# The rows of a gather and the gate products of one Trainium2 core's expert layer: a fixed order between them on VectorE, fetches paced by copied row numbers, and gate reads queued behind tile loads

## The chip, the cores and the metric

The kernel runs on one of the eight cores of a Trainium2 chip. The metric is the device time of one execution in microseconds (us), here the median of several runs. A core has five engines with a queue each: TensorE (PE in the profile, with its weight loads PEld), VectorE (DVE), ScalarE (ACT), GpSimd (POOL) and SyncE (SP). An engine works through its own queue in order; engines wait for each other by semaphores. Transfers are issued from the queues of SP, ACT and POOL.

## The reference

One layer of a decoder with 512 tokens of width 1024: an mLSTM and sliding-window attention mixer, cross-attention into 256 memory tokens, and a product-key expert layer. Only the last matters here. Each of 8 heads takes its best 16 of 128 x 128 single-neuron experts:

```python
u = expert_down[eidx]                                  # (token, head, 16, D)
a = gelu(einsum('thkd,td->thk', u, xb))
coef = softmax(top_s) * a
out = einsum('thk,thkd->td', coef, expert_up[eidx])
```

There are 16384 experts, each a row of 1024 numbers in `expert_down` and one in `expert_up`; 8 x 16 = 128 of them are chosen for a token. The layer's result is added to the residual, and a final RMSNorm gives the output. Everything is float32.

## The kernel before, in words

The 512 tokens are four blocks of 128. The kernel handles two kinds of block differently.

*Blocks 1 to 3 (384 tokens) go through all experts.* The 16384 experts are 128 tiles of 128. A "down tile" (class `Down`, lines 812 to 859) loads the tile's rows (`draw`, two tiles per transfer, line 820), splits them on ScalarE into a rounded part `dh` (line 785) and on VectorE into a remainder `dl` (line 823), multiplies in 24 matmuls (lines 834 to 836) and takes a gelu. An "up step" (`up_tile` and `up_mm`, lines 862 to 909) multiplies that gelu with the gates: it loads the tile of `expert_up` (`uraw`, line 876), splits it into `uh` (ScalarE, line 785) and `ul` (VectorE, line 886), forms the product `cf` of gelu and gates on VectorE (line 893), splits the product into `ch` (ScalarE, line 895) and `cl` (VectorE, line 896), and accumulates 18 matmuls (lines 907 to 909) into six banks that stay open over all 128 steps. All these working tiles have two buffers. The first SP = 72 down tiles are made early, among the routing and the gating, and are spilled to memory (`gd`); seven more (LEAD) are made between the gating and the up steps; the other 49 are made among the up steps, at a rate that `made_by` sets, so that a step has none or one of them. With FREE = 3 the matmuls of a down tile may not be queued ahead of those of the up step three before.

*The gates* are a table of token by expert in memory, `wd`, one per block. For block 1 GpSimd adds 128 columns into it, one indirect transfer each (`scatter`, line 685). For blocks 2 and 3 the function `gating` (lines 694 to 750) builds it on chip: for 32 groups q of four tokens, one-hot matrices come from VectorE (line 739) and ScalarE, TensorE multiplies them (line 740), ScalarE copies the result into a staging tile `stg` (line 742, two buffers), and after every eighth group ScalarE's queue stores it (line 744, 2 MB each). The early down tiles' matmuls run between. An up step reads the gates of four tiles at a time as `wt`, in three transfers from SP's queue (line 868), one for each block.

*Block 0 (128 tokens) gathers its rows.* For each of its 128 (head, rank) pairs j, GpSimd fetches 128 rows, one for each token, by an indirect transfer (line 762, 512 KB). `gather` (lines 753 to 779) is a generator of 256 rounds: the first 128 fetch from `expert_down` and take a dot product on VectorE (line 768), then the coefficients are formed, and 128 more fetch from `expert_up` and add to `gacc` on VectorE (line 778). Below, a "row" is one such round, numbered 0 to 255, and its VectorE instruction is the "row operation". Rows use eight buffers, so a fetch waits for the row operation eight before. The row numbers come from `eidx`, or from its copy `rowid` after LEAD.

*What sets the order.* The program is built by a scheduler that fixes each engine's queue ahead of time. Among instructions that its own timeline holds to be ready it takes the one that the program names first. `issue_after(x)` forces the instructions of one engine that follow in its block to be queued behind x on that engine; it is an order and no semaphore. By hand, 12 rows are placed in the gating of block 3 (at q = 9, 11, ... 31, set GQ), 10 in LEAD (GLD), and the other 234 among the up steps: line 1185 gives each step a due number, 3 for a step plus 5 for each down tile made, and line 1186 shares the rows out in proportion, up to step GST - 1 = 119. A row's operation is queued behind the step's product (the first row) or behind its `cl` (the others), which bounds it on one side alone: nothing forces it ahead of later steps.

After the last step, `finish` (lines 912 to 927) adds `gacc` (block 0) and the open banks (blocks 1 to 3) to the residual, takes the norm on VectorE, ScalarE and GpSimd, and stores the output. The last two steps' matmuls are taken block by block.

Of the kernel before, what the change touches and what calls it, by code (L numbers as in the profile page):

```python
# [21 lines left out]
P = 128  # L22
# [18 lines left out]
UG = 4  # L41
# [8 lines left out]

GQ = range(9, 32, 2)
GLD = 10
GST = 120
WST, WTL = 3, 5


# [637 lines left out]
def gating(c, early, ga):  # L694

    nc, ps, gs, mp = c.nc, c.ps, c.gs, c.mp
    V, A, T = nc.vector, nc.scalar, nc.tensor
    for b in range(NG + NS, NB):
        tr = []
        for n_, src in (("I1T", c.I1), ("I2T", c.I2), ("gT", c.gg)):  # L700
            tp = ps.tile([P, 512], F32, tag="a", name="tp_i")
            tr_ = T.transpose(tp[:, :P], src[:, b].rearrange("p h k -> p (h k)"), c.ident)
            o = gs.tile([P, P], F32, tag=n_, bufs=1, name=n_)
            A.copy(o, tp[:, :P])
            tr.append(o)
        i1, i2, g = tr
        n1 = gs.tile([P, P], F32, tag="n1", bufs=1, name="n1")
        A.mul(n1, i1, -1.0)
        io = c.iota.unsqueeze(1).to_broadcast([P, 4, P])

        def onehot(q):

            o1 = gs.tile([P, 4, P], F32, tag="oh1", bufs=5, name="oh1")
            ib = i1[:, 4 * q:4 * q + 4].unsqueeze(2).to_broadcast([P, 4, P])
            if q % 2:
                V.tensor_tensor(o1, io, ib, op=ALU.is_equal)
            else:
                for t1 in range(4):
                    t = 4 * q + t1
                    A.activation(o1[:, t1], c.iota, AF.Abs, bias=n1[:, t:t + 1])  # L720
                A.activation(o1, o1, AF.Relu, bias=1.0, scale=-1.0)
            return o1

        oh = [onehot(q) for q in range(3)]
        if b == NG + NS:
            with c.tc.issue_after(tr_.ins):
                early.fill(FGT0)
        for q in range(32):
            if q % 8 == 0:
                stg = gs.tile([P, NK, 32], F32, tag="stg", bufs=2, name="stg")  # L730
            if q + 3 < 32:
                oh.append(onehot(q + 3))
            o1 = oh[q]
            w = ps.tile([P, 512], F32, tag="b", name="w")
            w4 = w.rearrange("p (i t) -> p i t", t=4)
            for t1 in range(4):
                t = 4 * q + t1
                o2 = gs.tile([P, P], F32, tag="oh2", bufs=4, name="oh2")
                last = V.tensor_scalar(o2, c.iota, i2[:, t:t + 1], g[:, t:t + 1], op0=ALU.is_equal, op1=ALU.mult)
                mm = T.matmul(w4[:, :, t1], o1[:, t1], o2, start=True, stop=True)  # L740
            q8 = q % 8
            A.copy(stg[:, :, 4 * q8:4 * q8 + 4], w4)
            if q8 == 7:
                nc.scalar.dma_start(c.wd[b - NG][:, :, 32 * UG * (q // 8):32 * UG * (q // 8 + 1)].rearrange("g p i -> p g i"),
                                  stg.rearrange("p (g i) t -> p g (i t)", i=UG))
            with c.tc.issue_after(mm.ins):
                early.fill(FGT)
            if b == NB - 1 and q in GQ:
                with c.tc.issue_after(c.sc[HD - 1][-1].ins), c.tc.issue_after(last.ins):
                    step(ga, 1)  # L750


def gather(c):

    nc, gp, mp = c.nc, c.gp, c.mp
    V, A, G = nc.vector, nc.scalar, nc.gpsimd
    dots = gp.tile([P, P], F32, name="dots")
    c.gacc = gp.tile([P, D], F32, name="gacc")

    def fetch(src, j):  # L760
        r = gp.tile([P, D], F32, tag="rows", bufs=8, name="rows")
        G.indirect_dma_start(out=r, out_offset=None, in_=src,  # L762
                             in_offset=bass.IndirectOffsetOnAxis(ap=c.rowid[:, j:j + 1], axis=0))
        return r

    for j in range(P):
        r = fetch(c.a["down_r"], j)
        V.tensor_tensor_reduce(r, r, c.xn0, 1.0, 0.0, op0=ALU.mult, op1=ALU.add, accum_out=dots[:, j:j + 1])  # L768
        yield
    coef = gp.tile([P, P], F32, name="coef")  # L770
    A.activation(coef, dots, AF.Gelu)
    V.tensor_tensor(coef, coef, c.gg[:, 0].rearrange("p h k -> p (h k)"), op=ALU.mult)
    for j in range(P):
        r = fetch(c.a["up"], j)
        if j == 0:
            V.tensor_scalar(c.gacc, r, coef[:, j:j + 1], None, op0=ALU.mult)
        else:
            V.scalar_tensor_tensor(c.gacc, r, coef[:, j:j + 1], c.gacc, op0=ALU.mult, op1=ALU.add)  # L778
        yield


def split3(c, pool, raw, tag, bufs):
# [29 lines left out]
class Down:  # L812


    def __init__(self, c, i2):
        nc, dp = c.nc, c.dp
        self.c, self.i2 = c, i2
        if i2 % GRP == 0:
            c.draw = dp.tile([P, GRP, D], F32, tag="draw", bufs=2, name="draw")
            nc.sync.dma_start(c.draw, c.a["down_t"][i2 // GRP])  # L820
        raw = c.draw[:, i2 % GRP]
        self.hi, self.lo = split3(c, dp, raw, "d", 2)
        c.dl = nc.vector.tensor_tensor(self.lo, raw, f32(self.hi), op=ALU.subtract)  # L823
        self.acc = None
        self.k = 0
# [36 lines left out]
def up_tile(c, u, i2, gel, acc):  # L862
    nc, up = c.nc, c.up
    V, A, T = nc.vector, nc.scalar, nc.tensor
    if i2 % UG == 0:
        c.wt = up.tile([P, ND, UG * P], F32, tag="wt", bufs=2, name="wt")
        for b in range(ND):
            i = nc.sync.dma_start(c.wt[:, b], c.wd[b][i2 // UG])
            for j in c.sc[HD - 1] if b == 0 else ():
                c.tc.add_manual_dep(i.ins, j.ins.name, SYNC, reason="gates complete")  # L870
        if i2 < SP:
            c.gsr = c.gl.tile([P, UG, TD], F32, tag="gsr", bufs=2, name="gsr")
            nc.sync.dma_start(c.gsr, c.gd[i2 // UG])
    if i2 % GRP == 0:
        c.uraw = up.tile([P, GRP, D], F32, tag="uraw", bufs=3, name="uraw")
        nc.sync.dma_start(c.uraw, c.a["up"].rearrange("(i p) d -> p i d", p=P)[:, i2:i2 + GRP])
    g = c.gsr[:, i2 % UG] if i2 < SP else gel[i2]
    raw = c.uraw[:, i2 % GRP]
    last = u == NK - 1
    if last:  # L880
        z = c.xlo.rearrange("p k t -> p (k t)")
        hi, lo = z[:, 0:D], z[:, D:2 * D]
        A.copy(hi, raw)
    else:
        hi, lo = split3(c, up, raw, "u", 2)
    V.tensor_tensor(lo, raw, f32(hi), op=ALU.subtract)  # L886
    cf = up.tile([P, TD], F32, tag="cf", bufs=2, name="cf")
    if last:
        ch, cl = z[:, 2 * D:2 * D + TD], z[:, 3 * D:3 * D + TD]
    else:  # L890
        ch = up.tile([P, TD], F32R, tag="ch", bufs=2, name="ch")
        cl = up.tile([P, TD], F32R, tag="cl", bufs=2, name="cl")
    c.cf = V.tensor_tensor(cf.rearrange("p (b t) -> p b t", t=32), g.rearrange("p (b t) -> p b t", t=32),
                    c.wt.rearrange("p b (q i t) -> p (b q) i t", q=4, i=UG)[:, :, i2 % UG], op=ALU.mult)
    A.copy(ch, cf)  # L895
    c.cl = V.tensor_tensor(cl, cf, f32(ch), op=ALU.subtract)  # L896
    return hi, lo, ch, cl
# [206 lines left out]
def body(tc, a, out, dbg=None):  # L1104
# [3 lines left out]
    with ExitStack() as st:  # L1108
# [55 lines left out]
            ws.close()  # L1164
        c.gl = st.enter_context(pool("gels"))
        with pool("gather", side="right") as c.gp:
            c.rowid = c.eidx
            ga = gather(c)
            with pool("gating") as c.gs:
                gating(c, early, ga)  # L1170
            c.up = st.enter_context(pool("up"))
            assert len(gel) == SP

            for n in range(LEAD):
                ahead(1)
                with tc.issue_after(c.dl.ins):
                    step(ga, GLD * (n + 1) // LEAD - GLD * n // LEAD)
            c.rowid = c.gp.tile([P, P], I32, name="rowid")
            with tc.issue_after(c.dl.ins):
                nc.vector.tensor_copy(c.rowid, c.eidx)  # L1180
            pst_ = [c.ps.tile([P, 512], F32, tag=t, name="acc_u") for t in "bbbbaa"]
            acc = [[pst_[2 * b], pst_[2 * b + 1]] for b in range(ND)]
            last, mms = [], []
            g0 = len(GQ) + GLD
            due = [WST * u + WTL * made_by(u) for u in range(-1, GST)]
            rows = [(2 * P - g0) * (d - due[0]) // (due[-1] - due[0]) for d in due]
            rows += [rows[-1]] * (NK - GST)
            for u, i2 in enumerate(up_order()):
# [6 lines left out]
                for i in range(rows[u + 1] - rows[u]):  # L1195
                    with tc.issue_after((c.cf if i == 0 else c.cl).ins):
                        step(ga, 1)
                if u >= NK - 2:
                    last.append(parts)
                else:  # L1200
                    for b in range(ND):
                        up_mm(c, u, parts, acc, b)
                    mms.append(c.mm)
# [34 lines left out]
def step(it, n):  # L1238
    for _ in range(n):
        next(it, None)  # L1240
# [49 lines left out]
```

## Time and profile before

| | us |
|---|---|
| median of 3 runs (1652.19 to 1653.87) | 1652.22 |
| the profiled execution | 1653.3 |
| its span, first to last instruction | 1651.5 |

| engine | busy us | share of the span |
|---|---|---|
| PE | 1609.7 | 97% |
| PEld (beside PE) | 1415.1 | 86% |
| DVE | 1235.1 | 75% |
| ACT | 723.6 | 44% |
| POOL | 591.1 | 36% |

The first 400 us or so are the mixer and the attention, then routing until about 680, the gating until about 870, LEAD until about 900 and the up steps until the end. The granted TensorE clock was 0.989 of full speed over the span. The profile comes from one execution. A timeline line reads: start and length in us, engine, line of the kernel, operation, output<-inputs, shapes, count, and in brackets the idle time just before with what ended it. A group line gives the count, busy us, mean ns of one, and the idle time of the engine before them. A wait line gives who waited for whom, the total in us, how often, and the longest. In the chain of waits each line is a start, a length and what the end of the program hung on then. SPq marks the time an instruction stood at the head of SyncE's queue.

### The profile page before, as it was taken

To read this page: it belongs to the slowest core of one execution; us is meant where nothing else is said; L and a number is where in the kernel's file an instruction comes from. 1 tells how busy PE (TensorE), PEld (TensorE's weight loads), DVE (VectorE), ACT (ScalarE), POOL (GpSimd) and SP (SyncE) were. 2 spreads that over 40 slices of the span, in tenths; PEclk is the share of its full clock that TensorE was granted. 3 is DMA by queue.
4 is the path that set the end of the run, shared out by engine and by line. 5 is a ranking of instruction groups with operands and counts; after the bars stand their busy time and mean duration, and the time that the engine had idled before them with its cause. 6 is when DMAs were issued, how large, how long until landed. Compare 5 with 4: busy or idle time off the path is not lost.

```text
span 1651.5 us, 23090 instructions
## 1 busy us (share of the span) xinstructions
PE 1609.7 (97%) x8388; PEld 1415.1 (86%) x8388; DVE 1235.1 (75%) x2704; ACT 723.6 (44%) x1217; POOL 591.1 (36%) x427
## 2 busy tenths in 40 slices
PE   8998899999999999999999999999999999999994
PEld 5776688878999999999998888888888888888883
DVE  5546564464787887777796888788888888888898
ACT  5445544342544454678664333333333333333332
POOL 2000000000027787877221543444433434334451
PEclk9999999999999999999999999999999999999997
DMA  5236134232254435678999999999989889988895
GB/s 214 77 127 255 59 126 173 77 153 106 96 168 145 116 71 141 181 190 213 342 305 339 410 393 347 343 342 338 334 335 367 338 321 333 362 317 320 323 364 181
DMA packets 151122, 402.17 MB, mean 244 GB/s; under 512 B 28368, under 2 KB 62304, under 8 KB 138848
## 3 DMA queue, kind: packets, MB, share of 16 engines
q1 hardware_dynamic: 58208, 240.04, 39.0%
q0 software_dynamic: 55360, 134.32, 24.8%
q10 hardware_dynamic: 37440, 26.35, 5.1%
q8 instruction: 66, 1.08, 0.3%
q14 instruction: 48, 0.39, 0.1%
HBM read 357.07 MB, written 43.58 MB: 243 GB/s over the span
## 4 chain that ended last, share of the span: by engine, by line
PE 89%; DVE 4%; DMA 3%; ACT 2%; issue 1%; POOL 0%; DVEq 0%; SPq 0%; POOLq 0%; ACTq 0%
PE acc_u L907 10%; PE acc_u L908 10%; PE acc_u L909 10%; PE acc_d L836 10%; PE acc_d L834 10%; PE acc_d L835 10%; PE acc_f L1008 4%; PE acc_f L1009 4%; PE acc_f L1010 4%; PE w L740 3%; DMA wd<-stg 3%; PE acc_t L1023 2%; PE acc_t L1022 2%; PE acc_t L1021 2%; DVE gacc L778 1%
## 5 line engine op out<-in xcount | busy, mean ns | idle before, releaser
L834 PE MATMUL acc_d<-xhi,dh 128*128 128x384 f32 x1024 | 349.8, 342 | 1.0 <-ACT gsp L856 1.0
L836 PE MATMUL acc_d<-xhi,dl 128*128 128x384 f32 x1024 | 345.0, 337 | 1.7 <-DVE dl L823 1.7
L835 PE MATMUL acc_d<-xlo,dh 128*128 128x384 f32 x1024 | 343.6, 336 | 0.0
L908 PE MATMUL acc_u<-ul,ch 128*128 128x512 f32 x762 | 297.7, 391 | 0.0
L909 PE MATMUL acc_u<-uh,cl 128*128 128x512 f32 x762 | 296.6, 391 | 0.0
L685 POOL DMA_INDIRECT wd<-gg,ei x128 | 231.6, 1810 | 147.6 <-DVE ei L679 84.8
L907 PE MATMUL acc_u<-uh,ch 128*128 128x512 f32 x762 | 264.4, 390 | 0.2 <-ACT ch L895 0.2
L762 POOL DMA_INDIRECT rows<-in_up_dram,rowid x128 | 169.4, 1323 | 236.8 <-DVE gacc L778 208.9
L823 DVE TENSOR_TENSOR dl<-draw,dh 128x1024 fp32r<-128x1024 f32 x128 | 156.1, 1220 | 92.8 <-ACT dh L785 90.3
L895 ACT CAST ch<-cf 128x384 fp32r<-128x384 f32 x127 | 65.1, 514 | 356.3 <-issue 339.2
L785 ACT CAST dh<-draw 128x1024 fp32r<-128x1024 f32 x128 | 134.0, 1049 | 195.6 <-PE acc_d L835 170.8
L762 POOL DMA_INDIRECT rows<-in_down_r_dram,rowid x106 | 142.6, 1346 | 199.1 <-DVE dots L768 158.4
L834 PEld LDWEIGHTS acc_d<-xhi,dh 128*128 128x128 f32 x1024 | 192.8, 188 | 5.3 <-ACT gsp L856 1.3
L836 PEld LDWEIGHTS acc_d<-xhi,dl 128*128 128x128 f32 x1024 | 192.6, 188 | 3.9 <-DVE dl L823 2.6
L835 PEld LDWEIGHTS acc_d<-xlo,dh 128*128 128x128 f32 x1024 | 192.8, 188 | 3.7
L909 PEld LDWEIGHTS acc_u<-uh,cl 128*128 128x128 f32 x762 | 143.0, 188 | 29.4
L908 PEld LDWEIGHTS acc_u<-ul,ch 128*128 128x128 f32 x762 | 143.0, 188 | 28.7
L907 PEld LDWEIGHTS acc_u<-uh,ch 128*128 128x128 f32 x762 | 142.9, 188 | 28.3 <-ACT ch L895 0.5
L886 DVE TENSOR_TENSOR ul<-uraw,uh 128x1024 fp32r<-128x1024 f32 x127 | 154.8, 1220 | 12.5 <-ACT uh L785 12.3
L778 DVE SCALAR_TENSOR_TENSOR gacc<-rows,coef,gacc 128x1024 f32<-128x1024 f32 x127 | 162.6, 1280 | 0.9
L768 DVE CUSTOM_DVE_ANT_0 rows<-rows,xn 128x1024 f32<-128x1024 f32 x128 | 153.7, 1218 | 0.0
L896 DVE TENSOR_TENSOR cl<-cf,ch 128x384 fp32r<-128x384 f32 x127 | 70.7, 557 | 86.4 <-ACT ch L895 79.9
(344 smaller groups left out, 2654.0 us busy)
## 6 DMA issues: line engine op xcount, KB each, us to landing
draw<-in_down_t_dram SPq DMA_DIRECT2D x64, 1024.0 KB
uraw<-in_up_dram SPq DMA_DIRECT2D x64, 1024.0 KB
wt<-wd SPq DMA_DIRECT2D x96, 256.0 KB
wd<-stg ACTq DMA_DIRECT2D x8, 2048.0 KB
gd<-gsp SPq DMA_DIRECT2D x18, 768.0 KB
gsr<-gd SPq DMA_DIRECT2D x18, 768.0 KB
wd<-zero ACTq DMA_DIRECT2D x1, 8192.0 KB
raw<-in_w_pq_dram SPq DMA_DIRECT2D x8, 1024.0 KB
```

Source lines behind the costliest of these rows:

```text
L685: i = G.indirect_dma_start(out=out, out_offset=bass.IndirectOffsetOnAxis(ap=ei[:, h, k:k + 1], axis=0), in_=c.gg[:, NG, hh, k:k + 1], in_o ...
L762: G.indirect_dma_start(out=r, out_offset=None, in_=src, in_offset=bass.IndirectOffsetOnAxis(ap=c.rowid[:, j:j + 1], axis=0))
L768: V.tensor_tensor_reduce(r, r, c.xn0, 1.0, 0.0, op0=ALU.mult, op1=ALU.add, accum_out=dots[:, j:j + 1])
L778: V.scalar_tensor_tensor(c.gacc, r, coef[:, j:j + 1], c.gacc, op0=ALU.mult, op1=ALU.add)
L823: c.dl = nc.vector.tensor_tensor(self.lo, raw, f32(self.hi), op=ALU.subtract)
L834: T.matmul(acc[:, :TD], self.hi[:, ks], c.xhi[:, k, NG * P:], start=(k == 0), stop=False)
L835: T.matmul(acc[:, :TD], self.hi[:, ks], c.xlo[:, k, NG * P:], start=False, stop=False)
L836: T.matmul(acc[:, :TD], self.lo[:, ks], c.xhi[:, k, NG * P:], start=False, stop=(k == KT - 1))
L886: V.tensor_tensor(lo, raw, f32(hi), op=ALU.subtract)
L907: T.matmul(acc[b][n], ch[:, t], hi[:, d], start=st, stop=False)
L908: T.matmul(acc[b][n], ch[:, t], lo[:, d], start=False, stop=False)
L909: c.mm = T.matmul(acc[b][n], cl[:, t], hi[:, d], start=False, stop=sp)
```

## The change

Four edits:

1. *The binding.* The product `cf` of up step u is queued on VectorE behind the last row operation of step u - 2 (GLAG = 2). The rows are shared out up to step 123 instead of 119 (GST).
2. *Row numbers by copies.* The first 22 rows take their numbers from a new table `rid`. VectorE copies one column of `eidx` into it at a time: 16 in the gating of block 3, behind the one-hots of q = 1, 3, ... 31, and 6 in LEAD, behind the `dl` of its first six tiles. GpSimd's fetch j waits for copy j.
3. *Gate reads.* Every `wt` transfer is queued on SP behind the last `draw` load of LEAD.
4. Bookkeeping for these: the last row operation, the last `draw` load and the number of copies are remembered.

```diff
-GST = 120
+GST = 124
+GI = range(1, 32, 2)
+GLAG = 2
...
             with c.tc.issue_after(mm.ins):
                 early.fill(FGT)
+            if b == NB - 1 and q in GI:
+                with c.tc.issue_after(last.ins):
+                    row_number(c)
...
-                             in_offset=bass.IndirectOffsetOnAxis(ap=c.rowid[:, j:j + 1], axis=0))
+                             in_offset=bass.IndirectOffsetOnAxis(
+                                 ap=(c.rid if src is c.a["down_r"] and j < len(GQ) + GLD else c.rowid)[:, j:j + 1], axis=0))
...
+def row_number(c):
+    n = c.nid
+    if n < len(GQ) + GLD:
+        c.nc.vector.tensor_copy(c.rid[:, n:n + 1], c.eidx[:, n:n + 1])
+        c.nid += 1
...
-            i = nc.sync.dma_start(c.wt[:, b], c.wd[b][i2 // UG])
+            with c.tc.issue_after(c.lead.ins):
+                i = nc.sync.dma_start(c.wt[:, b], c.wd[b][i2 // UG])
...
-    c.cf = V.tensor_tensor(cf.rearrange("p (b t) -> p b t", t=32), g.rearrange("p (b t) -> p b t", t=32),
-                    c.wt.rearrange("p b (q i t) -> p (b q) i t", q=4, i=UG)[:, :, i2 % UG], op=ALU.mult)
+    with c.tc.issue_after(c.gate[max(u - GLAG, 0)].ins if c.gate else c.cl.ins if u else c.dl.ins):
+        c.cf = V.tensor_tensor(cf.rearrange("p (b t) -> p b t", t=32), g.rearrange("p (b t) -> p b t", t=32),
+                               c.wt.rearrange("p b (q i t) -> p (b q) i t", q=4, i=UG)[:, :, i2 % UG], op=ALU.mult)
...
             for n in range(LEAD):
                 ahead(1)
                 with tc.issue_after(c.dl.ins):
+                    row_number(c)
                     step(ga, GLD * (n + 1) // LEAD - GLD * n // LEAD)
+            c.lead = c.draw_dma
...
                 for i in range(rows[u + 1] - rows[u]):
                     with tc.issue_after((c.cf if i == 0 else c.cl).ins):
                         step(ga, 1)
+                c.gate.append(c.row)
```

More of the change, by code (lines that the diff above doesn't have):

```diff
@@ L767, in gather @@
         r = fetch(c.a["down_r"], j)
-        V.tensor_tensor_reduce(r, r, c.xn0, 1.0, 0.0, op0=ALU.mult, op1=ALU.add, accum_out=dots[:, j:j + 1])
+        c.row = V.tensor_tensor_reduce(r, r, c.xn0, 1.0, 0.0, op0=ALU.mult, op1=ALU.add, accum_out=dots[:, j:j + 1])
         yield
@@ L777, in gather @@
         else:
-            V.scalar_tensor_tensor(c.gacc, r, coef[:, j:j + 1], c.gacc, op0=ALU.mult, op1=ALU.add)
+            c.row = V.scalar_tensor_tensor(c.gacc, r, coef[:, j:j + 1], c.gacc, op0=ALU.mult, op1=ALU.add)
         yield
+def row_number(c):
[3 more added lines that the diff above has]
+        c.nid += 1
 def split3(c, pool, raw, tag, bufs):
@@ L819, in __init__ @@
             c.draw = dp.tile([P, GRP, D], F32, tag="draw", bufs=2, name="draw")
-            nc.sync.dma_start(c.draw, c.a["down_t"][i2 // GRP])
+            c.draw_dma = nc.sync.dma_start(c.draw, c.a["down_t"][i2 // GRP])
         raw = c.draw[:, i2 % GRP]
@@ L1166, in body @@
         with pool("gather", side="right") as c.gp:
-            c.rowid = c.eidx
+            c.rid = c.gp.tile([P, len(GQ) + GLD], I32, name="rid")
+            c.nid = 0
             ga = gather(c)
@@ L1172, in body @@
             assert len(gel) == SP
+            g0 = len(GQ) + GLD
             for n in range(LEAD):
@@ L1176, in body @@
                 with tc.issue_after(c.dl.ins):
+                    row_number(c)
                     step(ga, GLD * (n + 1) // LEAD - GLD * n // LEAD)
+            assert c.nid == g0
+            c.lead = c.draw_dma
             c.rowid = c.gp.tile([P, P], I32, name="rowid")
@@ L1182, in body @@
             acc = [[pst_[2 * b], pst_[2 * b + 1]] for b in range(ND)]
-            last, mms = [], []
-            g0 = len(GQ) + GLD
+            last, mms, c.gate = [], [], []
             due = [WST * u + WTL * made_by(u) for u in range(-1, GST)]
```

## The prediction

> **What bounds the kernel now.** I read the page first, then busy time by stretches, the waits of TensorE, the chain of waits, and VectorE's groups and timeline where the chain leaves TensorE. The profiled execution took 1653.3 us: this span and 1.8 us around it. The median of the three runs is 1652.2, so I sum against 1653.3 and give the result 1.1 lower.
>
> ```profile
> span 1651.5 us, 23090 instructions
> ```
> ```profile
> 913.00:1616.00 703.00, 703.00 (x3353) 614.11 (x3352) 584.27 (x742) 246.47 (x339) 299.51 (x225) 1.00 0.92 345
> 1616.00:1630.10 14.10, 14.09 (x63) 11.32 (x61) 13.75 (x14) 2.83 (x4) 3.69 (x3) 1.00 0.75 236
> 1630.10:1651.50 21.40, 0.00 (x0) 0.00 (x0) 15.08 (x28) 5.12 (x16) 2.16 (x4) 0.56 0.37 139
> ```
>
> The columns are the stretch, its length, then PE, PEld, DVE, ACT and POOL busy (instructions), granted clock, DMA share, GB/s. For 703 us TensorE (PE) never pauses; VectorE (DVE) has 584 of 703 us of work, 83%. Then TensorE ends at 1630.1 and 21.4 us follow without it. So time can be won in the last 21.4 us, and in the gating, where TensorE's waits between 800 and 900 us are small:
>
> ```profile
> PE w L740 <- DVE oh L739: 2.0, 1, 2.0
> PE acc_d L834 <- ACT gsp L856: 1.0, 1, 1.0
> PE acc_d L836 <- DVE dl L823: 0.9, 2, 0.7
> ```
>
> The end, on VectorE:
>
> ```profile
> 1617.46 0.55 DVE L893 TENSOR_TENSOR cf<-gel,wt 128x384 f32<-128x384 f32 x1
> ...
> 1625.05 9.20 DVE L778 SCALAR_TENSOR_TENSOR gacc<-rows,coef,gacc 128x1024 f32<-128x1024 f32 x7
> 1634.29 1.29 DVE L920 TENSOR_TENSOR hb<-hb,gacc 128x512 f32<-128x512 f32 x2
> ...
> 1643.86 2.74 DVE L926 SCALAR_TENSOR_TENSOR hb<-hb,frst,xn 128x512 f32<-128x512 f32 x4 [0.60 <-POOL frst L938]
> ```
>
> The last seven row operations (one gathered row per token, L778) stand behind all else; the four final blocks wait for them, end at 1646.6, and 4.9 us later the span ends. Their data were not late:
>
> ```profile
> 1621.94 1.67 POOL L762 DMA_INDIRECT rows<-in_up_dram,rowid  x1 [0.66 <-DVE gacc L778]
> ```
>
> This is the last fetch; its operation is the seventh above, started at 1625.05 + 9.20 - 1.28 = 1632.97, so a fetch needs 11.0 us at most there. It is the order in which VectorE was given its work that puts these rows last. Over the main loop:
>
> ```profile
> L778 DVE SCALAR_TENSOR_TENSOR gacc<-rows,coef,gacc 128x1024 f32<-128x1024 f32 x116 | 148.5, 1280 | 0.7
> L886 DVE TENSOR_TENSOR ul<-uraw,uh 128x1024 fp32r<-128x1024 f32 x121 | 147.6, 1220 | 10.7 <-ACT uh L785 10.5
> L768 DVE CUSTOM_DVE_ANT_0 rows<-rows,xn 128x1024 f32<-128x1024 f32 x106 | 127.1, 1218 | 0.0
> ...
> L893 DVE TENSOR_TENSOR cf<-gsr,wt 128x384 f32<-128x384 f32 x70 | 38.7, 553 | 0.8
> L893 DVE TENSOR_TENSOR cf<-gel,wt 128x384 f32<-128x384 f32 x51 | 28.2, 554 | 0.7
> ```
> ```profile
> L893 DVE TENSOR_TENSOR cf<-gsr,wt 128x384 f32<-128x384 f32 x72 | 39.8, 553 | 0.8
> L893 DVE TENSOR_TENSOR cf<-gel,wt 128x384 f32<-128x384 f32 x55 | 30.2, 553 | 0.7
> ```
>
> The first fence covers 913.6 to 1613.3 us, the second 885 to 1616.2. Row operations hardly idle (0.7 and 0.0 us), yet the order hands out only 106 + 116 of them in 699.7 us, one per 3.15 us. With the one of another form (j = 0, L776) they are rows 22 to 244; row 244 belongs by the due list to step 111, while 72 + 55 = 127 products (cf) are issued, up to step 126. The rows have slid 15 steps behind.
>
> **The change, part by part.** *Binding.* The product of step u now stands behind the last row operation of step u - 2. A row is issued where the builder's own timeline believes its data are there; the slide shows that it believes in one row per 3.15 us, and before this cost nothing because products passed the rows. Bound, they cannot: behind a held product stand its correction cl and the next tile's splits, and TensorE waits for the product's cast ch. GST = 124 spreads the same 234 rows over 125 due dates instead of 121, so the last row (255) belongs to step 123 and precedes the product of step 125. Where the first row comes is read here:
>
> ```profile
> 872.65 0.71 SPq L820 DMA_DIRECT2D draw<-in_down_t_dram  x1
> 873.66 13.56 SPq L868 DMA_DIRECT2D wt<-wd  x3
> 887.26 0.95 SPq L876 DMA_DIRECT2D uraw<-in_up_dram  x2
> 888.25 0.47 SPq L820 DMA_DIRECT2D draw<-in_down_t_dram  x1
> ```
> ```profile
> 898.45 1.23 DVE L823 TENSOR_TENSOR dl<-draw,dh 128x1024 fp32r<-128x1024 f32 x1 [0.82 <-ACT dh L785]
> ...
> 901.88 0.22 DVE L1180 COPY rowid<-eidx 128x128 int32<-128x128 int32 x1
> ...
> 913.65 1.22 DVE L768 CUSTOM_DVE_ANT_0 rows<-rows,xn 128x1024 f32<-128x1024 f32 x1
> ```
>
> *Reads of gates behind tile loads.* The three wt reads hold SyncE 13.56 us for the last gate store, and the last LEAD load (draw) stands behind them at 888.25. Turned round, it goes up to 14.6 us sooner (between 873.66 and 888.25); its split (dl, 898.45) also needs a free buffer, so I take 9 us sooner, which brings rowid from 901.9 to 893 and row 22 from 913.7 to 904. Queued behind the draw are then wt and uraw; wt's third part waits for the store anyhow, so that costs 0 to 2 us.
>
> At 3.15 us a row, row 255 starts at 904 + 233 x 3.15 = 1638. Then come that row 1.28, a product 0.55 and its cast, then three steps on TensorE:
>
> ```profile
> 1576.90 0.51 ACT L895 CAST ch<-cf 128x384 fp32r<-128x384 f32 x1 [2.61 <-PE acc_u L908]
> 1577.32 1.05 ACT L785 CAST uh<-uraw 128x1024 fp32r<-128x1024 f32 x1
> 1580.98 0.52 ACT L895 CAST ch<-cf 128x384 fp32r<-128x384 f32 x1 [2.61 <-issue]
> ```
>
> A step without a down tile lasts 1580.98 - 1576.90 = 4.08 us, so TensorE ends at 1638 + 1.28 + 0.55 + 0.52 + 12.24 = 1652.6, not 1630.1: **+22.5**. The bounds of this term are 0 (on the chip the rows lie ready, VectorE has 17% to spare) and +22.5; a gain is excluded, since TensorE had no gap to win. I take the upper end because a second reckoning reaches it. Where a late row has pushed a product behind the split of the next step, the chain from TensorE's end of a step is uh 1.05, ul 1.22, row 1.28, cf 0.55, ch 0.52 = 4.62 us against 4.08: 0.54 lost, 1.82 with a second row in between, 3.1 with a third. The due list gives 1 row to plain steps and 3 to steps with a down tile; some 25 places at 0.5 to 1.8 make about as much.
>
> *The tail.* With all rows ahead of the last products, the final blocks no longer wait. The last one needs an add 0.65, a square with its sum 0.77, the power 0.53, two products of 0.69 and the 4.9 us:
>
> ```profile
> 1643.27 1.06 POOL L938 TENSOR_TENSOR frst<-rsq,mhalf 128x1 f32<-128x1 f32 x2 [2.72 <-DVE rsq L937]
> ```
> ```profile
> 1639.93 0.58 ACT L921 ACTIVATE acc_u<-hb 128x512 f32<-128x512 f32 x1
> 1640.45 0.19 ACT L921 ACTIVATION_READ_ACCUMULATOR acc_u<-hb 128x1 f32 x1
> ```
>
> That is 8.2; with some 0.3 for the one-column steps between and 1.1 for queueing behind the block before it (both estimates: a block has about 2.9 us of VectorE work, and TensorE ends blocks 2.7 us apart, 12 matmuls of 4.08 / 18) it is 9.6 instead of 21.4: **-11.8** (bounds -8 to -13).
>
> *Fetches spread.* Fetches 0 to 15 of the gating wait for number copies at every second group; six more come in LEAD. Eight bunched fetches no longer travel beside the gate store that lasts 26.80 us:
>
> ```profile
> 783.16 26.80 DMA wd<-stg
> ...
> 869.54 17.34 DMA wd<-stg
> ```
>
> That store precedes TensorE's 2.0 us wait. 22 copies of one column each cost less than the 0.22 us of the whole table, 0 to 5 us in all, under matrix work that runs on. GpSimd then waits for a copy with the next fetch queued behind it; the dots that use it come four row pairs later, but in LEAD the last follows its number by one tile (about 4 us), less than 11, so its reader may stand still some us. Net -2, between -4 and +4. [...]
>
> Sum: 1653.3 + 22.5 - 11.8 - 2 = 1662.0; on the median's scale **1661**.
>
> **Rivals.** *(1) The binding is free.* For it speaks that no row waits for data and that VectorE is 83% busy: it may catch up wherever the builder erred. Then 1653.3 - 11.8 - 2 = 1639.5, 1638 on the median's scale, faster. It decides if products still run before the splits of their steps. [...] As a mechanism: PEld is 614 of 703 us, so if TensorE could run 12% faster after a gap, losses of 22 us would be won back, and the time would be 1638 as well. The trace speaks against it: plain steps last 4.08 us with no idle in them. I give that 0.03 within the 0.37 of this rival. *(2) The binding costs as much as the tail gives*, about 14: within 0.2% of 1652. *(3) The binding costs more.* The products of steps 1 and 2 also wait for row 22; a late start adds up to 9 (no earlier rowid), and a builder that loses more than one row time per slip adds as much again: 1661 + 9 + 9 = 1679. *(4) The change does not do what it says:* the rows remain last because another wait holds them; then 1650 to 1652. The order of VectorE's queue is binding, so this is small.
>
> **How the numbers follow.** 0.2%, 3.3 us, is about what a measurement of this kernel can tell from no change. Forecast (1655.5 to 1670) 0.38; rival 1 0.37; rivals 2 and 4 together 0.11; rival 3 0.14. So faster 0.37, same 0.11, slower 0.52. The range goes from 1636 (rival 1 with the tail at -13) to 1679. The likeliest case's own range is 1655.5 to 1670.
>
> **What would show it.** Right: the rows stay within two steps of their products, TensorE has gaps in 913 to 1616 that wait for ch or cl, together about 20 us, and ends near 1652; after its end about 10 us follow. Wrong: TensorE still shows 703 of 703 and ends by 1630, which is rival 1; or the seven rows are still last, rival 4. For the gating, the store of 783 us lands before 805 and TensorE's 2.0 us wait for the one-hots is gone.

## The result, and the profile after

The changed kernel takes **1671.45 us** (median of 4 runs, 1667.33 to 1671.9), the kernel before 1652.2 (1649.59 to 1653.87): ratio **1.0112**, 95% interval 1.0092 to 1.0133, or +18.5 us. Forecast were +9. The direction was right, the size was not. The profiled execution took 1671.1 us, its span is 1669.4.

After, busy time by stretches (stretch, length, then PE, PEld, DVE, ACT, POOL busy with instructions in brackets, granted clock, DMA share, GB/s):

```profile
785.00:870.00 85.00, 84.61 (x575) 83.80 (x573) 71.13 (x195) 59.85 (x128) 28.88 (x17) 1.00 0.89 304
870.00:900.00 30.00, 21.63 (x120) 20.66 (x120) 15.58 (x24) 9.07 (x14) 7.63 (x5) 0.95 0.99 353
900.00:925.00 25.00, 19.18 (x79) 16.69 (x80) 16.36 (x25) 7.35 (x10) 12.09 (x10) 0.78 1.03 410
925.00:1616.00 691.00, 684.20 (x3252) 596.34 (x3251) 570.11 (x727) 241.41 (x329) 284.38 (x224) 1.00 0.93 344
1616.00:1658.10 42.10, 40.21 (x175) 32.26 (x173) 31.76 (x45) 16.07 (x29) 1.12 (x2) 1.00 0.36 135
1658.10:1669.40 11.30, 0.00 (x0) 0.00 (x0) 4.13 (x10) 1.34 (x4) 1.10 (x2) 0.66 0.36 138
```

The first three stretches before:

```profile
785.00:870.00 85.00, 83.05 (x557) 82.68 (x556) 69.39 (x174) 56.51 (x122) 19.76 (x18) 0.98 0.93 322
870.00:900.00 30.00, 27.91 (x148) 25.43 (x147) 20.69 (x29) 13.44 (x20) 1.67 (x1) 1.00 0.92 327
900.00:925.00 25.00, 25.00 (x129) 22.79 (x128) 19.85 (x31) 9.19 (x13) 15.28 (x12) 1.00 1.02 411
```

TensorE ends at 1658.1 instead of 1630.1, 28.0 later. Behind it follow 11.3 us instead of 21.4, so 10.1 come back. The 28.0: between 785 us and its end TensorE is idle for 0.39 + 8.37 + 5.82 + 6.80 + 1.89 = 23.3 us, before for 1.95 + 2.09 = 4.0, a difference of 19.2. Another 2.0 were lost ahead of the gating (its first store starts at 785.18 instead of 783.16). These are no effect of the change: in two kernels of the experiments whose edits all come behind the gating this store starts at 782.78 (the orders without the binding) and at 786.63 (both orders, a distance of six). About 3 are matmuls at a lower granted clock: 4.8 behind the waits of the changed kernel (the last section), less 1.6 behind the one wait of 2 us before (a clock of 0.60 over the 4 us from 815.9). The last 3 to 4 aren't placed. **More than half of the idle time, 14.2 us, lies between 870 and 925 us**, where LEAD ends and the up steps begin; call it the entry. The wide loop behind it loses 6.80 + 1.89 = 8.7.

The waits of TensorE after, first at the entry (885 to 925 us), then from 925 on:

```profile
PE acc_d L850 <- ACT dh L801: 11.2, 1, 11.2
PE acc_u L925 <- ACT ch L913: 1.8, 1, 1.8
```
```profile
PE acc_u L925 <- ACT ch L913: 6.8, 4, 1.9
PE acc_u L925 <- ACT uh L801: 1.4, 1, 1.4
PE acc_u L926 <- DVE ul L903: 0.5, 1, 0.5
```

The 11.2 us are down tile 78, the seventh and last of LEAD, which waits for its load. SyncE's queue shows why; the last line here is what its second line hung on:

```profile
871.45 0.63 SPq L836 DMA_DIRECT2D draw<-in_down_t_dram  x1
872.13 19.78 SPq L893 DMA_DIRECT2D uraw<-in_up_dram  x3
892.01 0.60 SPq L836 DMA_DIRECT2D draw<-in_down_t_dram  x1
892.93 5.14 SPq L885 DMA_DIRECT2D wt<-wd  x6
```
```profile
SPq L893 <- DMA wd<-stg: 17.6, 1, 17.6
```

The gate reads (wt) do stand behind the last LEAD load (draw), as the change asks. But the place that they left was taken by three uraw loads, one for each of its three buffers (the other working tiles have two). These must wait for the last gate store, like the gate reads before them, and they hold the draw until 892.01, where it was 888.25 before. Before, TensorE had the first up steps to do at this point, with the product of step 0 issued at 890.78; now this product stands behind the last split of LEAD, at 907.52, and the next two behind row 22. VectorE's timeline has what hangs on the late draw:

```profile
905.11 0.22 DVE L1203 COPY rowid<-eidx 128x128 int32<-128x128 int32 x1
...
918.04 1.21 DVE L776 CUSTOM_DVE_ANT_0 rows<-rows,xn 128x1024 f32<-128x1024 f32 x1
...
1633.63 1.28 DVE L786 SCALAR_TENSOR_TENSOR gacc<-rows,coef,gacc 128x1024 f32<-128x1024 f32 x1
```

rowid comes at 905.1 (forecast 893), row 22 at 918.0 (forecast 904), row 255 at 1633.6 (forecast 1638). The binding does what it says: no row is more than one step behind its product, before up to 15.

### The profile page after: what moved, and what is told of

It is laid out like the page before. It is cut to its first block, busy times and chain, and to the rows that moved or that the text cites. A ratio compares the mean times of both kernels' runs of the same rounds, so it can differ in the third digit from the quotient of the medians.

```text
span 1669.4 us, 23048 instructions
## 1 busy us (share of the span) xinstructions
PE 1618.9 (97%) x8388; PEld 1418.7 (85%) x8388; DVE 1231.0 (74%) x2726; ACT 727.2 (44%) x1217; POOL 586.9 (35%) x427
## 3 DMA queue, kind: packets, MB, share of 16 engines
q0 software_dynamic: 55360, 134.32, 24.5%
## 5 line engine op out<-in xcount | busy, mean ns | idle before, releaser
L850 PE MATMUL acc_d<-xhi,dh 128*128 128x384 f32 x1024 | 350.7, 343 | 12.2 <-ACT dh L801 11.2
L926 PE MATMUL acc_u<-ul,ch 128*128 128x512 f32 x762 | 291.1, 394 | 0.5 <-DVE ul L903 0.5
L927 PE MATMUL acc_u<-uh,cl 128*128 128x512 f32 x762 | 258.2, 391 | 0.0
L801 ACT CAST uh<-uraw 128x1024 fp32r<-128x1024 f32 x127 | 133.1, 1050 | 229.3 <-PE acc_u L927 183.7
L769 POOL DMA_INDIRECT rows<-in_down_r_dram,rowid x106 | 130.4, 1230 | 195.7 <-DVE dots L776 173.2
```

The lines of the kernel that those rows point to most:

```text
L769: G.indirect_dma_start(out=r, out_offset=None, in_=src, in_offset=bass.IndirectOffsetOnAxis(ap=(c.rid if src is c.a["down_r"] and j < len( ...
L801: c.nc.scalar.copy(hi, raw)
L850: T.matmul(acc[:, :TD], self.hi[:, ks], c.xhi[:, k, NG * P:], start=(k == 0), stop=False)
L926: T.matmul(acc[b][n], ch[:, t], lo[:, d], start=False, stop=False)
L927: c.mm = T.matmul(acc[b][n], cl[:, t], hi[:, d], start=False, stop=sp)
```

## The experiments

Ratios are to the kernel before, run on the same chip, with the 95% interval. "Alone" means the kernel before with that part of the change's diff and nothing else. Loop waits are added up from matmul start to matmul start, which makes each some 0.4 us longer than the idle time in the stretches.

**The change taken apart**

*The binding alone* (with GST = 124).

> The kernel before with the binding and the due list to step 123 alone. Theory A: waits of 10 to 13 us in the loop, the part behind TensorE's end 10 to 12 us instead of 21.4, TensorE's 2 us wait at 813 us still there: about 1655 (1651 to 1659). Theory B (binding costs 22.5): about 1663.

Ratio 1.0070 (1.0048 to 1.0092). The waits at the entry, then the stretches of loop and end:

```profile
PE acc_d L847 <- ACT dh L798: 4.2, 2, 3.9
PE acc_u L921 <- ACT ch L909: 1.1, 1, 1.1
PE acc_d L849 <- DVE dl L836: 0.6, 1, 0.6
```
```profile
925.00:1616.00 691.00, 679.53 (x3234) 591.04 (x3233) 567.24 (x721) 239.33 (x327) 294.21 (x222) 1.00 0.93 344
1616.00:1654.70 38.70, 36.82 (x160) 29.41 (x158) 29.19 (x43) 15.43 (x27) 1.12 (x2) 1.00 0.30 114
1654.70:1666.00 11.30, 0.00 (x0) 0.00 (x0) 4.14 (x10) 1.34 (x4) 1.10 (x2) 0.73 0.37 138
```

TensorE ends 24.6 us later than before, and 10.1 come back at the end. That is dearer than theory A said and near the predicted 22.5: the price came out about right, though not by the terms that the prediction gave for it (see below). The loop loses 11.47 + 1.88 = 13.4 us and the entry 5.9.

*The gate reads alone.*

> The kernel before with the gate-read edit alone. Theory A: uraw loads ahead of the last LEAD draw hold SyncE's queue until the last gate store has landed, TensorE waits 8 to 12 us there and runs slower for some tens of us behind it; the rows still slide to the end, so that the part behind TensorE's end stays near 21: about 1666 (1661 to 1670). Theory C (the wait is there only together with the copied row numbers, whose fetches lengthen the last gate store from 17 to 23 us): a wait under 5 us, 1652 to 1657.

Ratio 1.0019 (1.0007 to 1.0031). Here too three uraw loads go first, and the draw is issued at 890.05. TensorE waits 5.4 us for it, half of what the changed kernel shows. Theory C is nearer: something in the other edits doubles this wait. Which of them does it isn't settled by this run.

*The row numbers alone.*

> The kernel before with the copied row numbers alone. Theory E (entry: the extra waits between 885 and 925 us come from the binding's first clause, which queues the product of step 0 behind the last LEAD tile's split and those of steps 1 and 2 behind row 22, so that TensorE has no up step to do while a late tile load is on its way): without the binding the products of steps 0 and 1 fill the time, TensorE waits under 4 us there, the 2 us wait at 813 us is gone, and the time is 0.998 to 1.002 of before. Theory F (six fetches beside the last gate store cost 10 us by themselves, as they did beside the binding): 1.005 or more.

Ratio 1.0043 (1.0031 to 1.0055), between the two bounds: E is wrong, F nearly right. TensorE waits 5.9 us for the first uraw cast, row 22 starts at 923.5 us instead of 913.7, and the end is 26.0 instead of 21.4. So this edit, which the prediction put down as a gain of 2, **costs 7 us**.

```profile
PE acc_u L923 <- ACT uh L801: 5.9, 1, 5.9
```

*Everything but the gate reads.*

> The kernel after without the gate-read edit (the binding and the copied row numbers stay). Theory A: draw is again issued at about 888 us, TensorE waits under 3 us there, waits of the binding in the loop stay at 10 to 12 us, and the end is shorter by 10: about 1655 (1652 to 1660). Theory B: about 1663 to 1670, with more than 20 us of waits in the loop.

Ratio 1.0131 (1.0110 to 1.0152). Both theories are wrong: the draw comes at 892.32, TensorE waits 10.0 and 4.4 us at the entry. The row numbers thus cost some 10 us beside the binding (1.0070 to 1.0131). The gate-read edit on top of the two costs nothing that can be told: 1.0131 and 1.0112 lie within each other's intervals.

*The changed kernel with the uraw loads behind the draw as well.*

```diff
-        nc.sync.dma_start(c.uraw, ...)
+        with c.tc.issue_after(c.lead.ins):
+            nc.sync.dma_start(c.uraw, ...)
```

> The kernel after, with the uraw loads queued behind the last draw load of LEAD as well. Theory A (the loss is the gate-read edit: with the gate reads out of the way the scheduler put three uraw loads ahead of that draw, and they wait for the staging tile that the last gate store still reads): TensorE's wait of 11.2 us at 892 us goes, the low clock behind it goes (about 5 us), and the time falls from 1671 to about 1655 (1651 to 1659). Theory B (the loss is the binding, at 22.5 us as predicted; the wait at 892 us only takes the place of later waits): the row operations stay at one per 3.15 us, TensorE waits later instead, and the time stays above 1664.

Ratio 1.0134 (1.0111 to 1.0156), and theory A, with which I went into the experiments, falls. The draw does go 8.5 us sooner than before (879.77 against 888.25), the 11.2 us are gone, rowid is there at 894.18, as predicted. But TensorE then waits 17.8 us for the product of step 1. VectorE's queue:

```profile
909.18 1.23 DVE L904 TENSOR_TENSOR ul<-uraw,uh 128x1024 fp32r<-128x1024 f32 x1 [3.92 <-ACT uh L801]
921.38 1.23 DVE L839 TENSOR_TENSOR dl<-draw,dh 128x1024 fp32r<-128x1024 f32 x1 [10.97 <-ACT dh L801]
...
924.80 1.22 DVE L776 CUSTOM_DVE_ANT_0 rows<-rows,xn 128x1024 f32<-128x1024 f32 x1
...
925.94 1.02 DVE L912 TENSOR_TENSOR cf<-gel,wt 128x384 f32<-128x384 f32 x2
```

The products of steps 1 and 2 (cf x2) stand behind row 22 (the row operation at 924.80), because the binding says so; row 22 stands behind the split dl of tile 80, and that tile's draw, now far back on SyncE, lands only at 920. Before, the products of steps 0 to 5 had gone by then.

**The entry**

*The binding for steps 6 to 127 only*, so that the first six products are free as before:

```diff
-    with c.tc.issue_after(c.gate[max(u - GLAG, 0)].ins if c.gate else c.cl.ins if u else c.dl.ins):
+    with ExitStack() if u < 6 else c.tc.issue_after(c.gate[u - GLAG].ins):
```

> The binding alone, but only for the products of steps 6 to 127; those of steps 0 to 5 are free as before. Theory E: the waits between 885 and 925 us (5.6 in the binding alone) go, the loop's waits (about 16) stay, so the ratio to before falls from 1.007 to about 1.003 (1.001 to 1.005). Theory R (the rows run at a pace of their own, 3.08 us each from row 22, and the products wait for them wherever they do: what the entry gives, the loop takes): 1.006 to 1.008, with the loop's waits grown to over 20.

Ratio 1.0025 (1.0013 to 1.0037), as theory E says: the entry shows no wait over 1 us. Theory R falls, so the rows have no pace of their own; row 22 starts later than in the binding alone (913.6 against 912.2), yet row 255 comes 7 us sooner.

> The binding for steps 6 to 127 together with the copied row numbers, without the gate-read edit. Theory E: the waits of 10.3 and 4.7 us between 885 and 925 us shrink to under 4 together and the low clock there goes, ratio 1.002 to 1.006 instead of 1.013. Theory F: the waits stay, since the last gate store is late whatever the products do: 1.009 or more.

Ratio 1.0111 (1.0091 to 1.0131). With the copied row numbers beside it, freeing the first six products gives little: 4.9 us go to a late uraw cast, 4.4 to a product at 943. Theory F holds here. The entry has two causes, first products that are held and transfers that land late.

**What the row numbers do**

```diff
-                                 ap=(c.rid if src is c.a["down_r"] and j < len(GQ) + GLD else c.rowid)[:, j:j + 1], axis=0))
+                                 ap=(c.rid if src is c.a["down_r"] and j < 16 else c.rowid)[:, j:j + 1], axis=0))
```

> The kernel before with copied row numbers for the 16 fetches of the gating only. Theory F: the wait of 2 us at 813 us is gone, the last gate store takes 16 to 19 us, row 22 starts by 915 us: ratio 0.997 to 1.000, against 1.0043 with all 22 copies. Rival (the spread of the 16 costs by itself): 1.003 or more.

> The kernel after with copied row numbers for the 16 fetches of the gating only; the six copies in LEAD are left out, and those six fetches go when a row buffer is free, as before. Theory F (what the row numbers cost is that six fetches are pushed into the stretch of the last gate store, 868 to 891 us): the last gate store takes 16 to 19 us instead of 22.6, the waits between 885 and 925 us fall from 13.4 to under 6, ratio 1.004 to 1.007 instead of 1.011. Rival (the waits of the entry come from the binding's first clause whatever the fetches do): 1.009 or more.

Ratios 1.0030 (1.0020 to 1.0040) and 1.0137 (1.0120 to 1.0154): both outside theory F's ranges and inside the rivals'. Leaving out the six copies in LEAD doesn't help. GpSimd's fetches between 860 and 892 us, first before, then with all 22 copies (alone), then with 16 (POOL busy, count):

```profile
860.00:892.00 32.00, 4.08 (x4) 1.00 0.83 285
```
```profile
860.00:892.00 32.00, 10.24 (x7) 1.00 0.84 283
```
```profile
860.00:892.00 32.00, 8.08 (x7) 0.95 0.88 323
```

With 16 copies seven fetches still go in this stretch. Spreading the first 16 to one each 5 us leaves the last six no time before the last gate store. Before, this store lasts 17.34 us (the prediction's row); with all 22 copies, then with 16, it lasts:

```profile
866.86 20.36 DMA wd<-stg
```
```profile
869.26 24.62 DMA wd<-stg
```

The decisive run lets the copies go at groups 0 to 21 of the gating (`GI = range(22)`, none in LEAD), so that the fetches wait for buffers, as before:

> The kernel before with all 22 row numbers copied at groups 0 to 21 of the gating and none in LEAD, so that fetches wait for buffers as before and hardly for numbers. Theory F (the copies cost only by when they let the fetches go: with 22 copies spread to 889 us seven fetches lie beside the last gate store, before three): three or four fetches after 860 us, the last gate store as before, ratio 0.999 to 1.0015. Rival (the copies or the waits on them cost by themselves): 1.003 or more.

Ratio 1.0006 (0.9995 to 1.0016), with the fetches and the store as before:

```profile
860.00:892.00 32.00, 4.49 (x4) 1.00 0.83 281
```
```profile
871.06 17.64 DMA wd<-stg
```

The copies cost nothing that can be told. What costs is the time to which they move the fetches. By which way it costs isn't separated: the longest store (16 copies) isn't the dearest kernel, and with 22 copies the last fetched rows are late as well (row 22 at 923.5, an end of 26.0).

**The loop**

Most of the waits of 2 us in the changed kernel's loop had another cause than the predicted one. After, around TensorE's wait at 1391.1, VectorE, then ScalarE, then TensorE:

```profile
1388.55 1.23 DVE L903 TENSOR_TENSOR ul<-uraw,uh 128x1024 fp32r<-128x1024 f32 x1 [1.12 <-ACT uh L801]
1389.69 1.28 DVE L786 SCALAR_TENSOR_TENSOR gacc<-rows,coef,gacc 128x1024 f32<-128x1024 f32 x1
1390.89 0.55 DVE L911 TENSOR_TENSOR cf<-gsr,wt 128x384 f32<-128x384 f32 x1
```
```profile
1391.59 1.04 ACT L801 CAST uh<-uraw 128x1024 fp32r<-128x1024 f32 x1 [3.07 <-PE acc_u L927]
1392.54 0.51 ACT L913 CAST ch<-cf 128x384 fp32r<-128x384 f32 x1
```
```profile
1393.10 0.51 PE L925 MATMUL acc_u<-uh,ch 128*128 128x512 f32 x1 [1.59 <-ACT ch L913]
```

The product is there at 1391.44. Its cast ch stands on ScalarE behind uh of the step after it, and uh waits for TensorE to finish the step that still uses the buffer. So TensorE ends, then uh, then ch, and TensorE begins. It is the same at 1292.5 and 1308.4; at 1544.6 ch stands behind the cast dh of a down tile instead. Counted over ScalarE's order, uh of a step stands ahead of ch of the step before in 18 places in the changed kernel and in the binding from step 6, in 1 before. VectorE's chain (split, row, product) is in the picture as well.

*Only the last products bound*, GST = 120:

```diff
+    with ExitStack() if u < 96 else c.tc.issue_after(c.gate[u - max(7, 14 - (u - 96) // 4)].ins):
```

> The kernel before with a binding of steps 96 to 127 only, whose distance falls from 14 steps to 7, so that the last row precedes the product of step 126; the due list ends at step 119 as before. If the binding's gain (the tail) and its cost (waits in the loop and at the entry) can be had apart: entry as before, loop waits 2 to 8 us, the part behind TensorE's end 11 to 13 us instead of 21.4: ratio 0.994 to 0.999. If rows cannot come sooner than they do without holding TensorE as long as the tail gives: 1.000 or more.

Ratio 1.0037 (1.0024 to 1.0050): the second case, no gain. The end shrinks to 14.3, but TensorE waits 10.4 us in four places between 1579 and 1613. The same catching up in fewer steps costs about the same, within what these runs can tell.

*The split behind the product on VectorE, binding from step 6*:

```diff
-    V.tensor_tensor(lo, raw, f32(hi), op=ALU.subtract)
...
+    with c.tc.issue_after(c.cf.ins):
+        V.tensor_tensor(lo, raw, f32(hi), op=ALU.subtract)
```

> The binding alone for steps 6 to 127, and the split ul of a step queued on VectorE behind that step's product. Theory L (a loop wait of 2 us comes where a row stands between the split of the next tile and its product, a chain of 4.62 us against a step of 4.08; with the product ahead of the split no row stands there): the loop's waits fall from 13 to under 5, ratio from 1.0025 to about 0.997 (0.995 to 0.999). Theory R (a product held for rows costs the same in any order): 1.001 to 1.004.

Ratio 1.0010 (1.0000 to 1.0020). Loop waits 9.5 instead of 14.8 us: a part, not the 5 that theory L gave.

*The casts in order on ScalarE*, in the changed kernel (shown) and, from step 7 on, in the binding from step 6:

```diff
-        hi, lo = split3(c, up, raw, "u", 2)
+        with c.tc.issue_after(c.ch.ins) if u >= 1 else ExitStack():
+            hi, lo = split3(c, up, raw, "u", 2)
...
-    A.copy(ch, cf)
+    c.ch = A.copy(ch, cf)
```

> The kernel after with one order more: on ScalarE the cast uh of a step is queued behind the cast ch of the step before. Theory Q (the waits of about 2 us in the loop come on ScalarE: the program was ordered as if the held product came late, so uh of step u stands ahead of ch of step u - 1, and uh waits for TensorE to free its buffer, while the product has been ready on the chip): the five waits of 1.8 to 2.3 us between 1290 and 1623 us shrink to 1.0 us or less each, 11 in all to under 5, ratio 1.006 to 1.009 instead of 1.011. Theory L (the product itself comes late, behind split and row on VectorE): the waits stay, 1.010 or more.

> The binding alone for steps 6 to 127 with the same order on ScalarE. Theory Q: loop waits fall from 14.8 to under 8, ratio from 1.0025 to 0.996 to 1.000. Theory L: 1.002 or more.

Ratios 1.0081 (1.0060 to 1.0102) and 1.0055 (1.0035 to 1.0076). The first lies in theory Q's range, but by other waits than it named: two of the five are 1.0 us, one of 1.75 stays, and a new one of 4.8 comes at 1189; most of the gain is at the entry, and the interval overlaps that of the changed kernel. The second is a plain miss: loop waits stay at 14.9. There, in seven of the nine waits for ch, it starts 0.09 us behind the product, which is now itself late; in the other two, at 1140 and 1530, it stands behind the cast dh of a down tile. Each order alone leaves waits to the other engine.

*Both orders, and the down tile's casts behind ch too*, binding from step 6:

```diff
-                    with tc.issue_after(mms[u - FREE].ins):
+                    with tc.issue_after(mms[u - FREE].ins), tc.issue_after(c.ch.ins) if u >= 7 else ExitStack():
```

> The binding alone for steps 6 to 127, the split ul behind the step's product on VectorE, and on ScalarE both uh and the down tile's casts behind the cast ch of the step before. If L and Q each hold in part: loop waits under 4 us instead of 9.5, the part behind TensorE's end 11 us, ratio 0.994 to 0.998, below both kernels. If the loop's cost comes back in another wait: 1.000 to 1.003.

Ratio **0.9958** (0.9944 to 0.9971), 1646.6 us: faster than both kernels, as expected. Waits from the entry on, and stretches:

```profile
PE acc_u L924 <- ACT ch L910: 2.5, 3, 1.0
PE acc_u L924 <- ACT uh L798: 1.4, 1, 1.4
PE acc_d L849 <- DVE dl L836: 0.6, 1, 0.6
```
```profile
925.00:1616.00 691.00, 687.68 (x3281) 600.19 (x3281) 581.19 (x738) 242.41 (x332) 290.94 (x224) 1.00 0.93 351
1616.00:1636.30 20.30, 20.20 (x90) 16.38 (x88) 14.52 (x25) 9.54 (x20) 1.12 (x2) 1.00 0.08 29
1636.30:1647.60 11.30, 0.00 (x0) 0.00 (x0) 4.07 (x10) 1.34 (x4) 1.10 (x2) 0.58 0.36 135
```

The loop now loses 3.4 us of idle time (before 0, the binding alone 13.4; from start to start 4.4, where under 4 was expected) and the end still gives 10.1. What the down tile's casts add to the two orders isn't known, since no run has the two without them.

> A control: the kernel before with the two orders of the version that was faster (split ul behind the step's product; uh and the down tile's casts behind the cast ch of the step before), but without the binding and with the due list to step 119. If the gain of that version is the binding's shorter end, which the two orders only make affordable: the seven rows are last again, 21 us follow TensorE's end, ratio 0.999 to 1.002. If the orders alone save time in the loop: 0.997 or less.

Ratio 1.0011 (1.0001 to 1.0021): without the binding the orders save nothing, the rows are last again. The gain needs the binding; the binding alone, from step 6, costs 0.25%, so it needs the orders too.

> The version with both orders and a binding with more room: the product of step u behind the last row of step u - 6, for steps 8 to 127, due list to step 121. If room takes away the waits that are left (4.4 us) while the last row still comes ahead of the last products: 0.992 to 0.996. If the rows come too late for the end again: 0.997 or more.

Ratio 0.9955 (0.9937 to 0.9973), no wait in the loop, an end of 13.1: no better than a distance of two, within the interval.

> The two together: 16 copied row numbers, the binding for steps 6 to 127, the split behind the product; no gate-read edit. If F and L both hold: 0.994 to 0.998. If L falls and F holds: 1.000 to 1.003. If F falls: 1.005 or more.

Ratio 1.0034 (1.0021 to 1.0046): L in part, F wrong for 16 copies; the entry takes what the loop gives.

## Why the prediction was wrong

**The failed step** is above all *Fetches spread*, "Net -2" in the sum: alone it costs 7.1 us (0.43%), beside the binding some 10. The gate reads failed too: they entered the sum as a gain, row 22 at 904 by a rowid at 893, with a cost of "0 to 2 us" that the sum left out; alone they cost 3.1 us (0.19%), and row 22 came at 918. With the binding's 0.70%, 11.6 us, the three make 21.8; together they measure 18.5. The sum had a flaw of its own as well: it took the 2 us of the gating off an end that it had reckoned from the rows, and by that reckoning a gain in the gating counts only where it brings row 22 forward.

- *The binding, +22.5 and the tail, -11.8, sum +10.7*: measured +11.6. The tail gave 10.1. That it came so near is luck, for the way to 22.5 was wrong in three terms that cancel: in the binding alone row 22 starts at 912.2, not 904 (+8); 233 rows take 718 us, not 734 (-16); TensorE ends 24.5 us after row 255 starts, not 14.6 (+10). In the changed kernel the three are +14, -18 and +10 (918.0, 716 and 24.4 us). Nor do rows set the pace, as the run that is bound from step 6 shows. Gaps of "together about 20" in 913 to 1616 were 8.7 after 925 in the changed kernel and 13.4 in the binding alone; the rest was at the entry, which the prediction mentions only as a part of rival 3.
- *The mechanism in the loop*: VectorE's chain of 4.62 us is one part of it; with the product ahead of the split the loop's waits fell from 14.8 to 9.5 us. The other part is ScalarE's order of casts, on which the prediction spent no line, though it quotes ch and uh side by side; with both in order, and the down tile's casts too, they fell to 4.4.
- *Reads of gates*: the step took "queued behind the draw are then wt and uraw" for granted. The edit orders only wt; the builder put uraw, which waits for the same store, into the place that came free. When uraw is moved too, the predicted 9 us appear (8.5) and are worth nothing, since the first products are bound to row 22 and this to a later tile.
- *Fetches spread*: right at 813 us, where the 2.0 us wait is gone. Wrong at 869: the step asked which store the fetches leave and not which one they join. The number that gave it away was in the trace of before: 22 rows through eight buffers, with four fetches from 860 to 892 us. With seven fetches in its stretch instead of four, the last gate store took 20.36 and 24.62 us instead of 17.34; how fetches and store get into each other's way isn't shown. But where the fetches go in time decides what they cost: moved to the last gate store 7 us, moved earlier nothing that can be told.
- *Rivals*: 1 (free) and 4 fall with the binding alone, and so does 2: the binding cost TensorE 24.6 us, and the tail gave 10.1. Nor does TensorE win gaps back by running faster behind them, as a part of rival 1 had it: in the binding alone it loses 5.9 + 13.4 us to gaps, and its end moves by more than that, 24.6. Rival 3 named the place (products of steps 1 and 2 behind row 22) and a time, 1679, nearer than the forecast's.

That the parts together cost 3 us less than their sum is no finding: it lies within their intervals (3.6, 2, 2 and 3.4 us to either side).

## What to carry to other kernels

An order that is forced on one instruction can leave a place in the queue (here three uraw loads took it and held the draw until 892.01 us): look at what else waits for the same event and will take it. A transfer that is taken out of one crowd can join another (here seven fetches beside the last gate store instead of four); ask which, and who waits there. Where a product is bound behind other work, see that its cast and the casts around it stand in the same order on their engine, and leave the first few steps free, whose data still come.

## What the runs showed of the hardware

Behind short waits of TensorE the granted clock fell at some places of these runs (to 0.50, 0.58 and 0.64) and not at others (1.00), and the length of the wait alone didn't decide it. The first 4 us behind a wait of 4.7 us (everything but the gate reads, from 923.7), and behind one of 2.26 us and one of 1.98 us in the changed kernel (from start to start):

```profile
923.70:927.70 4.00, 3.98 (x9) 3.15 (x10) 4.00 (x8) 0.49 (x1) 2.26 (x3) 0.50 1.03 420
```
```profile
1292.50:1296.50 4.00, 3.97 (x11) 3.12 (x12) 4.00 (x5) 0.00 (x0) 1.01 (x1) 0.58 0.92 317
...
1308.40:1312.40 4.00, 4.00 (x17) 3.29 (x18) 4.00 (x5) 0.00 (x0) 1.10 (x2) 1.00 0.79 285
```

But two waits of the same idle time, 2.57 us, first in the binding from step 6, then in the changed kernel with 16 copies, left different clocks behind them (0.58 and 1.00):

```profile
1296.66 0.80 PE L921 MATMUL acc_u<-uh,ch 128*128 128x512 f32 x1 [2.57 <-ACT ch L909]
```
```profile
1296.70:1300.70 4.00, 4.00 (x11) 3.21 (x12) 4.00 (x6) 0.01 (x1) 1.31 (x2) 0.58 0.69 248
```
```profile
1311.48 0.50 PE L925 MATMUL acc_u<-uh,ch 128*128 128x512 f32 x1 [2.57 <-ACT ch L913]
```
```profile
1311.50:1315.50 4.00, 4.00 (x18) 3.33 (x19) 4.00 (x6) 0.00 (x0) 1.29 (x2) 1.00 0.60 194
```

So the same wait cost its length in the changed kernel with 16 copies, and about 1.7 us more in the binding from step 6 (4 x 0.42, an estimate from the clock of 0.58). What decides it isn't shown. In the changed kernel this adds 4.8 us by the same estimate: 1.7 from 904 (0.57), 1.4 from 920 (0.64, behind a wait of 1.83 us of idle time) and 1.7 from 1292.5 (0.58).
